# Summing the last four modulation rows on GpSimd: two during the projections, two at half the pace in the attention

## The chip, the cores and the metric

The kernel runs on one core of a Trainium2 chip. The core has TensorE for matmuls (PE in the profile, its weight loads PEld), VectorE (DVE), ScalarE (ACT), GpSimd (POOL) and a queue on SyncE (SP) that here issues all the loads and stores around the change. Each engine works through its own instructions in the order in which the program wrote them. The metric is the device time of one execution in microseconds (us); lower is better.

## The reference

Three layers of a transformer at sequence length 1024 and width 1024. What matters here is the first layer's modulation and what uses it:

```python
mod = jax.nn.silu(c) @ w_ada[l] + b_ada[l]                # c: 1 x 1024, w_ada: 1024 x 6144
shift1, scale1, gate1, shift2, scale2, gate2 = jnp.split(mod, 6, axis=-1)
h = rms_norm(x, norm1_g[l]) * (1.0 + scale1[:, None, :]) + shift1[:, None, :]
z = h @ w_in[l]
c_q, c_kv, k_pe, dq, dk, dv = jnp.split(z, offsets, axis=-1)
...                                                       # MLA attention and differential attention
x = x + gate1[:, None, :] * mix
h2 = rms_norm(x, norm2_g[l]) * (1.0 + scale2[:, None, :]) + shift2[:, None, :]
```

The six rows of `mod` are numbered 0 to 5 in this order. Rows 0 and 1 are needed before the first projection; row 2 (gate1) at the end of the attention, rows 3 and 4 behind it, row 5 (gate2) later still.

## The kernel before

**How a row of the modulation is computed.** A row j needs eight tasks k = 0 to 7. A task loads a 128 x 1024 block of `w_ada` (512 KB, `ada_load`, L588), multiplies it by the column k of silu(c) on GpSimd (one tensor_scalar, L626) and adds it into the accumulator `acc` (`fine`, L335: four adds of 256 columns). Before task 0 the accumulator is zeroed (L582) and its first partition is loaded with the bias (L583). After task 7 TensorE adds up the 128 partitions with a matrix of ones (`ada_sum`, L598, two halves of 512 columns), ScalarE copies the two halves back (L315) and SP stores the row in `d_mod` (L618).

**Double buffers.** The weight blocks have two buffers. The load for task i + 1 is written into the program together with task i, and it overwrites the block of task i - 1. SP therefore waits there until GpSimd has added task i - 1, and everything that stands behind that load in SP's queue waits with it.

**Who sets the order.** `Pipe.feed` is one step of the pipeline: it advances every unit in its list once, in the order of the list, and each unit writes its instructions for that step. A `yield` ends a unit's part of the step. In this text the steps of the q and k projections are numbered: steps 0 to 7 are the calls with `d_unit(0, t)` (L815), steps 8 to 15 those with `d_unit(1, t)` (L828), t = 0 to 7. Ahead of step 0 come the calls with `d_unit(2, t)` (the v projection), behind step 15 those with `latent_unit(t)`.

**The projections** (`phase_z`). In its first step `d_unit(b, t)` writes 24 matmuls of 128 x 512 (L365) into one of four PSUM banks, the copy out of PSUM on ScalarE (L317 or L315) and four VectorE operations of `rope` (L770 to L774). Two steps later come the four transposes (L394) and the split of their result into a high and a low part (L341 on ScalarE, L342 on VectorE) in one of two staging buffers, and one step later the store to `d_dq` or `d_dk` (L795). The weights of the k block are loaded in step 0 by `w_block(1)` (L426, two pieces of 1 MB), ahead of anything that is appended behind `d_unit(0, 0)`. The weights of the latent block are loaded and split in steps 8 to 15. GpSimd has no instruction in the trace between the last row norm of the input and the first norm of the latents.

**The attention** (`phase_attn`). Each pass of the loop (L1163) feeds one `m_unit` and two `d_unit` steps. `ada_rest` is spawned at L1161, waits nine steps (3 * LAG) and then spends two steps on each of its 32 tasks (rows 2 to 5); the row sum is written four steps after the eighth add, by `finish`. Row 2 is read back as `gate` at L1166.

Of the kernel before, what the change touches and what calls it, by code (L numbers as in the profile page):

```python
# [10 lines left out]
F32 = mybir.dt.float32  # L11
# [3 lines left out]
OP = mybir.AluOpType  # L15
# [4 lines left out]
P = 128  # L20
S = 1024
D = 1024
NT = S // P
KD = D // P
# [11 lines left out]
LAG = 3  # L36
# [33 lines left out]
class Pipe:  # L70
# [1 line left out]


    def __init__(self):
        self.active, self.fresh, self.waiting = [], [], []

    def feed(self, *units):
        self.active.extend(self.fresh)
        self.fresh.clear()
        self.active.extend(units)  # L80
        for a in list(self.active):
            if next(a, StopIteration) is StopIteration:
                self.active.remove(a)
        for w in list(self.waiting):
            w[0] = [a for a in w[0] if a in self.active]
            if not w[0]:
                self.waiting.remove(w)
                w[1]()
# [205 lines left out]
def three_layer_kernel(ctx: ExitStack, tc: tile.TileContext, I, out, stop=99, dbg=None):  # L294
    nc = tc.nc
    V, A, G, T, SP = (GUARD(e) for e in (nc.vector, nc.scalar, nc.gpsimd, nc.tensor, nc.sync))
# [9 lines left out]
    go = Pipe()  # L306
# [6 lines left out]
    def acopy(dst, src, scale=None):  # L313
        if scale is None:
            A.activation(out=dst, in_=src, func=AF.Copy)  # L315
        else:
            A.activation(out=dst, in_=src, func=AF.Copy, scale=scale)  # L317
# [14 lines left out]
    def fine(out, a, b, op):  # L332

        for c in range(0, out.shape[-1], 256):
            G.tensor_tensor(out[:, c:c + 256], a[:, c:c + 256], b[:, c:c + 256], op=op)  # L335
# [78 lines left out]
    def weights(raws, parts, per=1):  # L414


        if not raws.rings:
            raws.reserve("raw", 2048)
        nb = len(raws.rings["raw"][0])
        q = []  # L420

        def load(i):
            hi, lo, src = parts[i][:3]
            raw = raws.tile([P, 2048], F32, name="raw")[:, :math.prod(hi.shape[1:])].rearrange(
                "p (k n) -> p k n", k=hi.shape[1])
            SP.dma_start(out=raw, in_=src)  # L426
            q.append(raw)

        for i in range(min(nb, len(parts))):
            load(i)  # L430
        yield
        yield
        for i in range(len(parts)):
            split_k(parts[i][0], parts[i][1], q[i], parts[i][3] if len(parts[i]) > 3 else None)
            if (i + 1) % per == 0 and i + 1 < len(parts):
                yield
            if i + nb < len(parts):
                load(i + nb)
# [4 lines left out]
    def new_weight(name, n):  # L443

        return [new_piece(name, q, n) for q in range(2)]

    def drop_weight(name):
        sb.drop(*[f"{name}{q}{nm}" for q in range(2) for nm in "hl"])

    def halves(pieces, src, c0, n):  # L450
        return [(*pieces[q], wsrc(src, 4 * q, 4, c0, n)) for q in range(2)]
# [42 lines left out]
    d_mod = dp.tile([6, D], F32, name="d_mod")  # L494
# [85 lines left out]
    def ada_acc(j, pl, e):  # L580
        acc = pl.tile([P, D], F32, name="acc", bufs=2)
        e.memset(acc, 0.0)  # L582
        SP.dma_start(out=acc[0:1], in_=I["b_ada"][0:1, j * D:(j + 1) * D])  # L583
        return acc

    def ada_load(pl, j, k):
        w = pl.tile([P, D], F32, name="adaw")
        SP.dma_start(out=w, in_=I["w_ada"][0][k * P:(k + 1) * P, j * D:(j + 1) * D])  # L588
        return w
# [4 lines left out]
    def ada_sum(acc, m=P):  # L594
        res = []
        for c in range(2):
            ps = p_tr.tile([P, 512], name="adaps")[0:m]
            T.matmul(ps, lhsT=ones[:, 0:m], rhs=acc[:, c * 512:(c + 1) * 512], start=True, stop=True)  # L598
            res.append(ps)
        return res  # L600

    def ada_rest():

        ad = Rings(sb, 2)
        todo = [(j, k) for j in range(2, 6) for k in range(KD)]
        w = ada_load(ad, *todo[0])
        accs = {}
        ad.reserve("acc", D, 2)
        for _ in range(3 * LAG):
            yield  # L610

        def finish(j):
            for _ in range(4):
                yield
            for c, ps in enumerate(ada_sum(accs[j], 1)):
                acopy(accs[j][0:1, c * 512:(c + 1) * 512], ps)
            yield
            SP.dma_start(out=d_mod[j:j + 1], in_=accs[j][0:1])  # L618
            if j == 5:
                ad.close()  # L620

        for i, (j, k) in enumerate(todo):
            w2 = ada_load(ad, *todo[i + 1]) if i + 1 < len(todo) else None
            if k == 0:
                accs[j] = ada_acc(j, ad, G)
            G.tensor_scalar(w, w, cc[:, k:k + 1], None, op0=OP.mult)  # L626
            yield
            fine(accs[j], accs[j], w, OP.add)
            w = w2
            yield  # L630
            if k == KD - 1:
                go.spawn(finish(j))

    def phase_z():
        zc = Rings(sb)
# [9 lines left out]
        def w_block(b):  # L645
            W[b] = new_weight(f"w{b}", 512)
            yield from weights(raws, halves(W[b], I["w_in"][0], 576 + 512 * b, 512))
# [14 lines left out]
        acc = [adap.tile([P, D], F32, name="acc", bufs=2) for _ in range(2)]  # L662
# [65 lines left out]
        for q in range(4):  # L728
            w = adap.tile([P, 2, 512], F32, name="adaw")
# [76 lines left out]
            go.feed(*([h_unit(i)] if i < NT else []), *([d_unit(2, i - 4)] if i > 4 else []))  # L806
        hb.close()
        drop_weight("w2")
        go.spawn(w_block(1))
        stg.reserve("qsb", 768)  # L810
        stg.reserve("kn", 512, 1)
# [109 lines left out]
        go.after(done)  # L921

    phase_z()
    if stop <= 1:
        go.drain()
# [51 lines left out]
    def phase_attn(wo, following):  # L977
# [29 lines left out]
        todo = Todo()  # L1007
# [150 lines left out]
        load_v("d", 0)  # L1158
        go.after(start_m)
        go.feed()  # L1160
        go.spawn(ada_rest())  # L1161
        seq = [(h, g, qi) for h in range(4) for g in range(4) for qi in range(2)]
        for i in range(len(seq) + LAG):  # L1163
            if i >= LAG:
# [764 lines left out]

    wo1 = OutWeights(I["w_out"][0], "wo")  # L1930
    w_units = phase_attn(wo1, lambda: open_w(wo1))
    if stop <= 2:
        go.drain()
# [453 lines left out]
```

## Time and profile before

| | us |
|---|---|
| median of 3 runs | 2597.66 |
| lowest and highest run | 2596.23, 2602.85 |
| the profiled execution | 2597.42 |
| span of its trace | 2595.7 |

| engine | busy us | share of the span |
|---|---|---|
| PE | 2461.7 | 95% |
| DVE | 1798.1 | 69% |
| ACT | 1458.0 | 56% |
| POOL | 557.7 | 21% |

The shares are averages over stages with different limits, so the stages are read one by one: the q and k projections, the latents, the attention. The rows below give times in us from the start of the span. In a timeline a row is a run of instructions of one line, with its start, its length, the count behind "x" and, in brackets, the idle time before it and what ended that. An engine's queue is marked with a q (SPq).

### The profile page before, as it was taken

How to read it: one execution, taken by the hardware profiler on the slowest of the kernel's cores; microseconds unless marked ns; L12 is line 12 of the kernel's file. 1: busy time of each engine (PE TensorE's matmuls, PEld its weight loads, DVE VectorE, ACT ScalarE, POOL GpSimd, SP SyncE). 2: the span in 40 equal slices, each digit the busy share in tenths (PEclk: the TensorE clock that was granted, in tenths of full speed). 3: DMA queues.
4: the chain of work that ended last, by engine and by line, in shares of the span. 5: the costliest groups of instructions: out<-in, count | busy, mean ns of one | idle time of the engine just before them, and what ended most of it. 6: DMA issues, size and time to landing. Idle time of an engine off the chain costs nothing. (4 is left out here: it accounts for less than half of the span.)

```text
span 2595.7 us, 37353 instructions
## 1 busy us (share of the span) xinstructions
PE 2461.7 (95%) x13658; PEld 2053.3 (79%) x13658; DVE 1798.1 (69%) x3072; ACT 1458.0 (56%) x2557; POOL 557.7 (21%) x523
## 2 busy tenths in 40 slices
PE   5999899998988999999997999999999899999999
PEld 3789788887876777777765887899999789888977
DVE  7654588887668999999998354536888436735952
ACT  3324577777217878878874343436888224435930
POOL 0000089936002222222211012310002002300400
PEclk8999999999989999999998999999999899999999
DMA  7355765553748999999968524337667324338523
GB/s 267 114 140 164 231 195 162 172 185 110 255 162 307 384 390 386 385 380 382 381 245 315 166 89 147 112 111 198 165 171 204 114 85 147 118 110 190 148 73 106
DMA packets 270416, 530.04 MB, mean 204 GB/s; under 512 B 28027, under 2 KB 180603, under 8 KB 244118
## 3 DMA queue, kind: packets, MB, share of 16 engines
q1 hardware_dynamic: 263062, 510.84, 60.0%
q0 software_dynamic: 7168, 16.79, 1.9%
q8 instruction: 109, 1.79, 0.3%
q14 instruction: 77, 0.63, 0.1%
HBM read 424.19 MB, written 111.76 MB: 206 GB/s over the span
## 5 line engine op out<-in xcount | busy, mean ns | idle before, releaser
L365 PE MATMUL ps<-t,t 128*128 128x512 f32 (+5 forms) x8224 | 1758.3, 370 | 3.8 <-DVE t L342 2.4
L365 PEld LDWEIGHTS ps<-t,t 128*128 128x128 f32 (+1 forms) x8224 | 1377.0, 182 | 313.0 <-DVE t L342 4.4
L342 DVE TENSOR_TENSOR t<-t,t 128x2048 fp32r<-128x2048 f32 (+4 forms) x226 | 472.3, 2115 | 55.3 <-ACT t L341 55.2
L341 ACT ACTIVATE t<-ps 128x512 fp32r<-128x512 f32 (+3 forms) x660 | 334.2, 544 | 313.9 <-PE ps L377 205.1
L342 DVE TENSOR_TENSOR t<-ps,t 128x512 fp32r<-128x512 f32 (+3 forms) x660 | 391.8, 623 | 89.7 <-ACT t L341 83.2
L341 ACT ACTIVATE t<-t 128x2048 fp32r<-128x2048 f32 (+4 forms) x226 | 399.9, 1773 | 31.0 <-DVE t L774 10.9
L322 POOL TENSOR_TENSOR small<-small 128x8 f32<-128x8 f32 (+3 forms) x120 | 137.3, 1145 | 944.8 <-DVE small L321 912.2
L317 ACT ACTIVATE t<-ps,small 96x512 f32<-96x512 f32 (+5 forms) x208 | 128.6, 618 | 322.8 <-PE ps L365 278.0
L335 POOL TENSOR_TENSOR t<-t,t 128x256 f32<-128x256 f32 (+1 forms) x224 | 166.3, 774 | 27.1 <-DMA t<-in_b_ada_dram 23.3
L315 ACT ACTIVATE t<-ps 128x256 f32<-128x256 f32 (+4 forms) x196 | 88.4, 453 | 125.0 <-PE ps L365 69.9
L377 PE MATMUL ps<-small,t 96*128 96x96 f32 (+1 forms) x736 | 94.3, 267 | 47.4 <-DMA t<-d_ye 18.0
L1512 POOL DMA_INDIRECT d_ye<-t,small x32 | 45.2, 1413 | 435.7 <-ACT t L317 429.1
L377 PEld LDWEIGHTS ps<-small,t 96*128 96x128 f32 (+1 forms) x736 | 82.4, 145 | 68.1 <-DVE t L1880 18.5
L2129 DVE TENSOR_TENSOR t<-t,ps 128x512 f32<-128x512 f32 x32 | 22.0, 688 | 125.8 <-PE ps L365 125.8
L2047 DVE CUSTOM_DVE_ANT_0 t<-ps,t 128x1024 f32<-128x1024 f32 (+7 forms) x128 | 95.5, 747 | 19.5 <-PE ps L2042 17.6
L349 DVE SCALAR_TENSOR_TENSOR t<-t,small,t 128x512 fp32r<-128x512 f32 (+5 forms) x124 | 80.2, 692 | 35.7 <-ACT t L348 35.7
L2051 ACT ACTIVATE t<-t,small 128x1024 f32<-128x1024 f32 (+7 forms) x128 | 99.3, 776 | 7.7 <-DVE small L2047 5.4
L626 POOL TENSOR_SCALAR t<-t,small 128x1024 f32<-128x1024 f32 x32 | 92.6, 2894 | 31.9 <-DMA t<-in_w_ada_dram 31.9
L1508 POOL DMA_INDIRECT t<-d_h,small x32 | 89.0, 2781 | 37.5 <-DVE small L1216 28.0
L1090 PE MATMUL ps<-t,t 128*128 128x512 f32 x320 | 83.6, 408 | 8.1 <-ACT t L1136 7.6
L1709 DVE TENSOR_REDUCE small<-t 128x8 f32<-128x512 f32 (+1 forms) x56 | 36.2, 647 | 79.0 <-ACT t L1708 79.0
L2066 PE MATMUL ps<-small,t 128*128 128x128 f32 x576 | 86.2, 277 | 0.4 <-ACT t L2051 0.3
(296 smaller groups left out, 2966.9 us busy)
## 6 DMA issues: line engine op xcount, KB each, us to landing
t<-in_w_expert_gate_dram SPq DMA_DIRECT2D x64, 1024.0 KB, 11.6
t<-in_w_expert_up_dram SPq DMA_DIRECT2D x64, 1024.0 KB, 11.1
t<-in_w_expert_down_dram SPq DMA_DIRECT2D x64, 1024.0 KB, 10.5
t<-in_w_ada_dram SPq DMA_DIRECT2D x48, 512.0 KB, 5.2
t<-d_ak SPq DMA_DIRECT2D x64, 256.0 KB, 4.7
t<-in_w_in_a_dram SPq DMA_DIRECT2D x12, 1024.0 KB, 9.1
t<-in_x_dram SPq DMA_DIRECT2D x16, 512.0 KB, 5.4
t<-d_dk SPq DMA_DIRECT2D x16, 512.0 KB, 8.7
```

The source lines that it names most:

```text
L315: A.activation(out=dst, in_=src, func=AF.Copy)
L317: A.activation(out=dst, in_=src, func=AF.Copy, scale=scale)
L322: G.tensor_tensor(dst, dst, mhalf[:, :dst.shape[-1]], op=OP.pow)
L335: G.tensor_tensor(out[:, c:c + 256], a[:, c:c + 256], b[:, c:c + 256], op=op)
L341: A.activation(out=hi, in_=src, func=AF.Copy)
L342: e.tensor_tensor(lo, src, f(hi), op=OP.subtract)
L365: T.matmul(ps, lhsT=a(k), rhs=b(k), start=(first and i == 0), stop=(last and i == n - 1))
L377: T.transpose(ps[:, k], src[:, (c + k) * P:(c + k + 1) * P], ident[:m, :m])
L626: G.tensor_scalar(w, w, cc[:, k:k + 1], None, op0=OP.mult)
L1508: G.indirect_dma_start(out=xg[e % 3], out_offset=None, in_=d_h2, in_offset=rows(idx_in[:CAP, e:e + 1]), bounds_check=S - 1, oob_is_err=False)
L2047: V.tensor_tensor_reduce(sbt[:, :n], ps[:, :n], c[:, :n], -1.0, 3e38, OP.add, OP.min, nm)
L2051: A.activation(out=pt[:, :n], in_=sbt[:, :n], func=AF.Exp, scale=-1.0, bias=nm, accum_out=RS[h][:, qt:qt + 1])
```

## The change

`Pipe` gets a second list, `side`. `feed` advances its units after all the active ones, so what they write stands behind the step's other instructions on each engine. `ada_rest` now takes the rows that it computes, a number of steps to wait at the start, and the number of steps that each task takes. It is called twice. For rows 2 and 3 it is appended just before step 0 of the projections, with no wait and one step for each task; `more=1` puts tasks 0 and 1 of row 2 into the same step, so that 16 tasks lie in steps 0 to 14. For rows 4 and 5 it is appended where `ada_rest` was before, with the same nine steps of waiting and four steps for each task. A task's product and its add are written into one step. There is one accumulator for both rows of a call. The row sum, its copies and the store of the row are written in the next step after the task with k = 7 (in the projections: steps 7 and 15), in front of the zeroing for the second row. The arithmetic of each task is as before.

```diff
@@ class Pipe
     def __init__(self):
-        self.active, self.fresh, self.waiting = [], [], []
+        self.active, self.fresh, self.waiting, self.side = [], [], [], []
@@ Pipe.feed
         for a in list(self.active):
             if next(a, StopIteration) is StopIteration:
                 self.active.remove(a)
+        for a in list(self.side):
+            if next(a, StopIteration) is StopIteration:
+                self.side.remove(a)
@@ three_layer_kernel
-    def ada_rest():
+    def ada_rest(js, start, pause, more=0):
 
         ad = Rings(sb, 2)
-        todo = [(j, k) for j in range(2, 6) for k in range(KD)]
+        todo = [(j, k) for j in js for k in range(KD)]
         w = ada_load(ad, *todo[0])
-        accs = {}
-        ad.reserve("acc", D, 2)
-        for _ in range(3 * LAG):
-            yield
-
-        def finish(j):
-            for _ in range(4):
-                yield
-            for c, ps in enumerate(ada_sum(accs[j], 1)):
-                acopy(accs[j][0:1, c * 512:(c + 1) * 512], ps)
-            yield
-            SP.dma_start(out=d_mod[j:j + 1], in_=accs[j][0:1])
-            if j == 5:
-                ad.close()
-
+        ad.reserve("acc", D, len(js) - more)
+        acc = ad.tile([P, D], F32, name="acc")
+        for _ in range(start):
+            yield
         for i, (j, k) in enumerate(todo):
             w2 = ada_load(ad, *todo[i + 1]) if i + 1 < len(todo) else None
             if k == 0:
-                accs[j] = ada_acc(j, ad, G)
+                G.memset(acc, 0.0)
+                SP.dma_start(out=acc[0:1], in_=I["b_ada"][0:1, j * D:(j + 1) * D])
             G.tensor_scalar(w, w, cc[:, k:k + 1], None, op0=OP.mult)
-            yield
-            fine(accs[j], accs[j], w, OP.add)
+            fine(acc, acc, w, OP.add)
             w = w2
-            yield
+            if i or not more:
+                for _ in range(pause):
+                    yield
             if k == KD - 1:
-                go.spawn(finish(j))
+                for c, ps in enumerate(ada_sum(acc, 1)):
+                    acopy(acc[0:1, c * 512:(c + 1) * 512], ps)
+                SP.dma_start(out=d_mod[j:j + 1], in_=acc[0:1])
+        ad.close()
@@ phase_z, ahead of go.spawn(w_block(1))
         drop_weight("w2")
+        go.side.append(ada_rest((2, 3), 0, 1, 1))
@@ phase_attn
-        go.spawn(ada_rest())
+        go.side.append(ada_rest((4, 5), 3 * LAG, 4))
```

## Rows read from the trace of the kernel before

**Rows 1.** Windows: projections, attention under ada_rest (length; busy PE, PEld, DVE, ACT, POOL; clock; DMA; GB/s)
```profile
84.00:190.00 106.00, 106.00 (x500) 87.77 (x499) 56.05 (x100) 27.08 (x44) 0.00 (x0) 1.00 0.43 123
330.00:546.00 216.00, 204.60 (x1257) 174.04 (x1258) 188.68 (x297) 167.88 (x325) 191.53 (x168) 0.99 0.64 188
```
**Rows 2.** Timeline of PE in the projections: steps 7 and 15 end, latents begin
```profile
137.24 5.74 PE L365 MATMUL ps<-t,t 128*128 128x512 f32 x24
142.82 0.60 PE L394 MATMUL ps<-small,t 128*128 128x128 f32 x4
...
190.15 0.60 PE L394 MATMUL ps<-small,t 128*128 128x128 f32 x4
190.51 6.63 PE L365 MATMUL ps<-t,t 128*128 128x288 f32 x48
```
**Rows 3.** POOL's groups by line from 320 to 560 us (busy us, mean ns | idle before)
```profile
L335 POOL TENSOR_TENSOR t<-t,t 128x256 f32<-128x256 f32 x128 | 96.0, 780 | 25.1 <-DMA t<-in_b_ada_dram 23.3
L626 POOL TENSOR_SCALAR t<-t,small 128x1024 f32<-128x1024 f32 x31 | 89.7, 2895 | 21.3 <-DMA t<-in_w_ada_dram 21.3
```
**Rows 4.** Timelines of POOL and SP where one modulation row ends, the next begins
```profile
375.50 2.81 POOL L335 TENSOR_TENSOR t<-t,t 128x256 f32<-128x256 f32 x4
378.25 0.96 POOL L582 MEMSET t<- 128x1024 f32 x1
379.18 2.86 POOL L626 TENSOR_SCALAR t<-t,small 128x1024 f32<-128x1024 f32 x1
...
382.70 2.82 POOL L335 TENSOR_TENSOR t<-t,t 128x256 f32<-128x256 f32 x4
...
379.23 0.25 SPq L583 DMA_DIRECT2D t<-in_b_ada_dram  x1
```
**Rows 5.** SP: timeline of the k weights' loads; summary of the q and k stores
```profile
98.53 1.71 SPq L426 DMA_DIRECT2D t<-in_w_in_dram  x2
...
L795 SPq EVENT_SEMAPHORE  x13: 17/17/17, 100.3 to 194.4; - x13
...
DMA to landing us min/median/max: 3.5/4.7/5.8
```
**Rows 6.** Windows, columns as in rows 1: the DMA while the k weights load
```profile
104.00:108.00 4.00, 4.00 (x22) 3.31 (x21) 0.87 (x2) 0.49 (x2) 0.00 (x0) 1.00 0.89 344
108.00:112.00 4.00, 4.00 (x19) 3.31 (x18) 3.80 (x5) 2.39 (x3) 0.00 (x0) 1.00 0.05 16
```
**Rows 7.** Timelines of PE and ACT: one row sum and its second copy
```profile
389.20 1.88 PE L598 MATMUL ps<-t,small 128*1 128x512 f32 x4
...
391.11 0.59 ACT L315 ACTIVATE t<-ps 1x512 f32<-1x512 f32 x1 [0.27 <-PE ps L598]
```
**Rows 8.** Windows, columns as in rows 1: the clock after PE had stood idle
```profile
309.00:319.00 10.00, 4.88 (x15) 3.78 (x16) 4.12 (x8) 4.70 (x8) 0.00 (x0) 0.52 0.96 292
```
**Rows 9.** Timeline of DVE in one step of the projections
```profile
108.13 0.76 DVE L770 TENSOR_TENSOR t<-t,t 128x256 f32<-128x256 f32 x2 [3.23 <-ACT t L317]
109.66 0.69 DVE L774 TENSOR_TENSOR t<-t 128x512 f32<-128x512 f32 x1
```
**Rows 10.** Timelines of DVE and POOL: one meeting, and the same DVE form alone
```profile
341.20 2.12 DVE L1150 SCALAR_TENSOR_TENSOR t<-t,small,t 128x1024 f32<-128x1024 f32 x1
566.05 1.28 DVE L1150 SCALAR_TENSOR_TENSOR t<-t,small,t 128x1024 f32<-128x1024 f32 x1
...
341.12 2.86 POOL L626 TENSOR_SCALAR t<-t,small 128x1024 f32<-128x1024 f32 x1
```
**Rows 11.** Timeline of DVE: row maximum of m_unit in passes 2, 22 and 28
```profile
343.33 1.23 DVE L1098 TENSOR_REDUCE small<-ps 128x1 f32<-128x1024 f32 x1
...
547.16 1.20 DVE L1098 TENSOR_REDUCE small<-ps 128x1 f32<-128x1024 f32 x1
...
606.25 1.20 DVE L1098 TENSOR_REDUCE small<-ps 128x1 f32<-128x1024 f32 x1
```
**Rows 12.** Waits of the SP queue from 288 to 560 us (total, times, longest)
```profile
SPq L588 <- POOL t L335: 140.6, 30, 8.0
```

## The prediction

> **What bounds the kernel now.** I read the windows by stage first. In the projections TensorE is busy without a gap, 106.00 of 106.00 us, VectorE half the time and GpSimd not at all; in the attention under ada_rest TensorE has 204.60 of 216.00, VectorE 188.68, and GpSimd 191.53 [rows 1]. So the projections are set by TensorE alone, and whatever makes it wait there comes out at the end in full; no later stage starts from anything else. The attention is close to TensorE's bound, with VectorE and GpSimd both near 90%. The timeline of PE gives the pace of the projections: a unit of 24 matmuls and 4 transposes starts every (190.15 - 142.82) / 8 = 5.92 us [rows 2]. The timeline of POOL gives the price of a modulation task, the SP rows when its first data can come, and the row maxima of m_unit the pace of the attention.
>
> **The price of a task, and the pace it is given.** 128 adds kept GpSimd busy 96.0 us, so 3.00 us for the four of one task; 31 products took 89.7 us, 2.89 each [rows 3]. A task is 5.89 us; undisturbed it is 2.81 + 2.86 = 5.7 [rows 4]. The change gives it 5.92 us (one step). That looks like a fit, but the first step holds two tasks, and the row sum stands only one step behind the eighth add: eight tasks must end within what TensorE needs for steps 0 to 7, counted from when the first data is there.
>
> **When GpSimd can start.** Step 0 is TensorE's work before step 1; the transposes at 142.82 follow step 7's matmuls, so step 7 is 137.24 to 142.82 [rows 2], and counting back it is 96 to 102 for step 0. Its SP instructions stand in this order: the last v store, the two 1 MB loads of the k weights, then the new loads. SP issues the k weights at 98.53 and is through at 100.3, where its next wait begins [rows 5]. Only then can it issue the first `w_ada` block. The DMA is moving the k weights at 344 GB/s until 108 and is empty behind it (16 GB/s) [rows 6]. The block queues behind them: 0.5 MB at 344 GB/s is 1.5 us more, so it is there at about 110. Bounds: 105 if it is served in between, 112 if bias and second block delay it. I take 110.
>
> **The new wait at step 7.** Eight tasks from 110: 110 + 8 x 5.89 = 157.1. In TensorE's queue the sum of row 2 stands behind step 7's matmuls, which end at 142.8. TensorE waits there 14.3 us, and every later matmul of the kernel is queued behind it. Part of it may show earlier: SP's load for task i + 1 waits for task i - 1, and the q store behind it waits too. The store of unit 0 would go out after the add of task 2 (110 + 3 x 5.89 = 127.7), land 4.7 us later [rows 5] at 132.4, and free the staging buffer that the split of step 4 (119.5) needs. ScalarE, held there, copies out the next banks late, and TensorE may wait some 5 us at the transposes of step 6. That wait lies inside the 14.3 us, since GpSimd does not depend on it.
>
> **The second row.** With one accumulator, GpSimd's zeroing for row 3 waits for the store of row 2, and all the later tasks stand behind it in its queue. After the eighth add: sum and two copies 391.11 + 0.59 - 389.20 = 2.5 us [rows 7]; the 4 KB store 0.25 us to issue and a landing that the trace doesn't show; zeroing 0.96 [rows 4]; product 2.89 and add 3.00. For the landing, the bias load of 4 KB issued at 379.23 was there by 382.70 [rows 4], so at most 3.5 us, and above 0; I take 2.5, nearer to the upper end, since the 512 KB stores took 3.5 to 5.8 [rows 5]. Together 12.1 us until row 3's first add is done, while the bias load hides behind the product. Seven more tasks: 41.2. So the eighth add of row 3 is done at 157.1 + 12.1 + 41.2 = 210.4. TensorE by itself is there at 157.1 + 1.9 [rows 7] + 8 x 5.92 = 206.4, and later by what the clock costs: in ten microseconds of which TensorE was busy for 4.88 the granted clock was 0.52, near the 1.2 GHz level [rows 8], and such a stretch loses 4.8 us; with a third of that it is 208, with all of it 211. Either way the sum of row 3 starts at about 210.5 and the latents at 212.4 instead of 190.5 [rows 2]. **The projections lose 21.9 us**, 3.8 of it the work of the two sums.
>
> What else moves here: 16 loads of 512 KB, two bias loads and two stores join SP's queue, all in front of the k stores and the latent weights' loads of the next step. The latent weights are needed only after step 15 and have some 3 us to spare by the same reckoning. VectorE's rope operations take 0.76 + 0.69 + 0.69 us a step, the third as the second [rows 9]; they will be lengthened by GpSimd as L1150 is, from 1.28 to 2.12 [rows 10]. Four such are at most 3.4 us, and rope ends at 109.66 + 0.69 = 110.35 where the transposes that need it come at 142.82 - 5 x 5.92 = 113.2: 2.9 us of cover. Costed at nothing; without cover, 0.5 us a step, and GpSimd is the later one anyway.
>
> **The attention.** Two of four sums leave it: -3.8 us [rows 7]. At half the density VectorE meets GpSimd half as often. Passes 2 to 22 lie under ada_rest and hold three sums: (547.16 - 343.33 - 3 x 1.88) / 20 = 9.91 us a pass; passes 22 to 28 hold one sum and none of the tasks: (606.25 - 547.16 - 1.88) / 6 = 9.54 [rows 7, 11]. All of the tasks cost 0.37 x 20 = 7.5 us; half of them gives back 3.7. Bounds: 0 and 7.5, with another 1 to 2 us since SP no longer stands 140.6 us waiting for adds [rows 12]: with four steps to a task the add that a load waits for is long done. The new sum stands four steps behind its add, and TensorE doesn't wait there.
>
> **The sum**, against the profiled execution (2597.4, 0.2 below the median, span 2595.7): 2597.4 + 21.9 - 3.8 - 3.7 = 2611.8, say **2612**.
>
> **A rule of the skill.** At 341.20 VectorE's L1150, with two inputs in SBUF, ran into a GpSimd product that began at 341.12 and ran 2.86 us; it took 2.12 us instead of 1.28 [rows 10] and ended at 343.32, before the product did. The Trainium skill, SBUF — State Buffer, "Who interferes with whom", says that the port shared by the two engines is an exclusive lock: the one that comes second is blocked until the first is through. This trace disagrees: the wait was 0.84 us, not 2.8.
>
> **Rivals.** (1) *VectorE's operations hold GpSimd back in full.* Each step has 0.76 + 0.69 + 0.69 = 2.14 us of rope [rows 9]; a task becomes 5.7 + 2.14 = 7.8 us, the sums come at 110 + 63 = 173 and 173 + 14 + 55 = 242, the latents at 244: +53.5 - 7.5, **2643**. Against it: in the attention, where VectorE was 87% busy, the task rose only from 5.7 to 5.89 [rows 3]. Chance 0.04. This is what the lock of the Trainium skill's page, SBUF — State Buffer, would do if VectorE always came first.
> (2) *The blocks come late.* SP's waits and the latents' loads stretch the task to 6.6 us, as the 21.3 us that 31 products waited for data in the attention would (0.7 each) [rows 3]: 110 + 53 = 163, + 12.8 + 46.2 = 222, latents at 224: +33.5 - 7.5, **2623**; at 7.0 us a task it is 2630. Chance 0.14.
> (3) *GpSimd keeps up, and the attention pays back: faster.* It decides at one point: if the eighth add is done by 142.8, TensorE doesn't wait. Then the sums only change places and the attention gains 3.7 to 9 us: **2589 to 2594**. That needs a start at 142.8 - 8 x 5.7 = 97 or before, and SP is through with the k weights only at 100.3 [rows 5]. Chance 0.05.
> (4) *A short wait and a large gain.* Start at 105, tasks of 5.7, store in 0.5 us: eighth adds at 151 and 201, TensorE itself at 202 with a little lost to the clock, latents at 204; +13.5 - 3.8 - 9 = **2598**; in between, no measurable difference. For it: the undisturbed pace does occur [rows 4]. Chance 0.11.
>
> **How the numbers follow.** The forecast has 0.66 and spans 2603 to 2619 by start (105 to 112), store and attention gain. What a measurement of this kernel can tell from no change is about 0.3%, 7.8 us, so faster is below 2589.9 and slower above 2605.5. Slower takes rivals 1 and 2 and nearly all of the forecast: 0.83; same takes rival 4, the lowest part of the forecast and part of rival 3: 0.13; faster, 0.04. The range runs from half of rival 4 to most of rival 2: 2600 to 2627.
>
> **What the profile would show.** PE with a wait at L598 for POOL's L335 near 143 and a second, shorter one near 205; the sum of the PE gaps up to the latents some 18 us; the latents beginning near 212; POOL back to back from about 110 with one hole of about 6 us between the rows; a lower granted clock behind the first wait; the passes of the attention at about 9.7 us. Wrong if L598 shows no wait, if POOL starts before 100, or if passes fall to 9.3.

## The result, and the profile after

The changed kernel took 2617.99 us (median of 4 runs, 2615.82 to 2618.84) against 2600.10 us for the kernel before on the same chip (4 runs, 2596.23 to 2602.85): ratio 1.0067, 95% interval 1.0053 to 1.0082. It is slower by 18 us; the forecast's sum has 14.4. The profiled execution took 2615.82 us, its span is 2614.1, which is 18.4 more than the span of before.

Line numbers moved by a few: the add is now L338 (L335 before), the product L619, the zeroing L617, the load L591, the row sum L601, the matmuls L368, the transposes L397, the q and k stores L792, rope's last operation L771, ScalarE's split L344, the row maximum L1096.

The timeline of PE through the projections, with the idle time and its releaser in brackets:

```profile
140.98 1.09 PE L397 MATMUL ps<-small,t 128*128 128x128 f32 x4 [9.38 <-DVE t L771]
141.72 7.50 PE L368 MATMUL ps<-t,t 128*128 128x512 f32 x24
...
149.41 5.70 PE L368 MATMUL ps<-t,t 128*128 128x512 f32 x24
159.36 3.45 PE L601 MATMUL ps<-t,small 128*1 128x512 f32 x4 [4.24 <-POOL t L338]
...
206.37 0.63 PE L397 MATMUL ps<-small,t 128*128 128x128 f32 x4 [1.99 <-DVE t L771]
206.75 7.33 PE L368 MATMUL ps<-t,t 128*128 128x512 f32 x24
...
218.33 3.57 PE L601 MATMUL ps<-t,small 128*1 128x512 f32 x4 [4.24 <-POOL t L338]
...
222.59 2.61 PE L368 MATMUL ps<-t,t 128*128 128x288 f32 x13
```

Each row sum is met by a wait in two pieces, one at the transposes of an earlier step (9.38, 1.99) and one at the sum itself (4.24 twice), 19.85 us together. The latents begin at 222.59, where it was 190.51 before [rows 2]: 32.1 us later.

The timeline of POOL shows why the sum comes so late:

```profile
109.98 2.86 POOL L619 TENSOR_SCALAR t<-t,small 128x1024 f32<-128x1024 f32 x1 [12.08 <-DMA t<-in_w_ada_dram]
112.92 3.98 POOL L338 TENSOR_TENSOR t<-t,t 128x256 f32<-128x256 f32 x4
116.89 3.29 POOL L619 TENSOR_SCALAR t<-t,small 128x1024 f32<-128x1024 f32 x1
120.26 4.49 POOL L338 TENSOR_TENSOR t<-t,t 128x256 f32<-128x256 f32 x4
...
157.70 2.97 POOL L338 TENSOR_TENSOR t<-t,t 128x256 f32<-128x256 f32 x4
164.79 0.95 POOL L617 MEMSET t<- 128x1024 f32 x1 [4.12 <-DMA d_mod<-t]
...
168.66 3.17 POOL L338 TENSOR_TENSOR t<-t,t 128x256 f32<-128x256 f32 x4
...
178.81 4.46 POOL L619 TENSOR_SCALAR t<-t,small 128x1024 f32<-128x1024 f32 x1
...
216.59 3.04 POOL L338 TENSOR_TENSOR t<-t,t 128x256 f32<-128x256 f32 x4
```

GpSimd starts at 109.98 (forecast 110) and then never waits for a block. Eight tasks end at 157.70 + 2.97 = 160.67, 6.34 us each; the zeroing waits 4.12 us for the store of row 2; the first add of row 3 is done at 171.83, the eighth at 219.63, so 47.8 / 7 = 6.83 us a task.

The timelines of SP and ACT show how the first wait came to stand at the transposes:

```profile
116.94 14.33 SPq L591 DMA_DIRECT2D t<-in_w_ada_dram  x3
131.37 0.53 SPq L792 DMA_DIRECT2D d_dq<-t  x1
...
136.99 0.60 ACT L344 ACTIVATE t<-ps 128x512 fp32r<-128x512 f32 x1 [16.54 <-DMA d_dq<-t]
```

SP sat at a `w_ada` load that needs an add done; the q store behind it left only at 131.37; ScalarE's split waited for the staging buffer, and VectorE's rope and TensorE's transposes waited for ScalarE.

In the attention, the windows from the row maximum of pass 2 to that of pass 22 and on to pass 28, for the kernel before and then for the changed one (the columns as in [rows 1]):

```profile
343.34:547.16 203.82, 194.62 (x1212) 166.60 (x1212) 178.89 (x282) 157.84 (x305) 179.54 (x158) 1.00 0.66 194
547.16:606.25 59.09, 58.09 (x365) 50.03 (x364) 50.26 (x87) 47.61 (x93) 19.68 (x26) 1.00 0.27 93
```

```profile
377.87:569.09 191.22, 189.47 (x1205) 165.90 (x1203) 165.21 (x281) 155.66 (x303) 96.10 (x83) 1.00 0.55 160
569.09:626.53 57.44, 56.71 (x366) 50.18 (x364) 50.08 (x84) 46.41 (x91) 19.11 (x25) 1.00 0.33 111
```

Pass 2 comes 34.5 us later than before, pass 28 only 626.53 - 606.25 = 20.3 later: the attention gives back 14.2 us, where 7.5 was forecast. Another 1.9 us went between there and the end of the span (20.3 to 18.4).

### The profile page after: what moved, and what is told of

Its sections match the earlier page's. It is cut to its first block, busy times and chain, and to the rows that moved or that the text cites. A ratio compares the mean times of both kernels' runs of the same rounds, so it can differ in the third digit from the quotient of the medians.

```text
span 2614.1 us, 37344 instructions
## 1 busy us (share of the span) xinstructions
PE 2468.4 (94%) x13658; PEld 2056.8 (79%) x13658; DVE 1798.1 (69%) x3072; ACT 1458.9 (56%) x2557; POOL 571.2 (22%) x523
## 5 line engine op out<-in xcount | busy, mean ns | idle before, releaser
L368 PE MATMUL ps<-t,t 128*128 128x512 f32 (+5 forms) x8224 | 1760.7, 371 | 4.5 <-DVE t L345 2.9
L368 PEld LDWEIGHTS ps<-t,t 128*128 128x128 f32 (+1 forms) x8224 | 1379.8, 183 | 313.5 <-DVE t L345 5.3
L344 ACT ACTIVATE t<-ps 128x512 fp32r<-128x512 f32 (+3 forms) x660 | 334.6, 544 | 352.4 <-PE ps L380 205.2
L344 ACT ACTIVATE t<-t 128x2048 fp32r<-128x2048 f32 (+4 forms) x226 | 400.0, 1774 | 47.3 <-DMA t<-in_w_in_dram 15.7
L338 POOL TENSOR_TENSOR t<-t,t 128x256 f32<-128x256 f32 (+1 forms) x224 | 178.2, 827 | 31.4 <-DMA t<-in_b_ada_dram 26.3
L380 PEld LDWEIGHTS ps<-small,t 96*128 96x128 f32 (+1 forms) x736 | 83.7, 147 | 67.3 <-DVE t L1878 18.6
L619 POOL TENSOR_SCALAR t<-t,small 128x1024 f32<-128x1024 f32 x32 | 95.2, 2975 | 22.7 <-DMA t<-in_w_ada_dram 22.7
## 6 DMA issues: line engine op xcount, KB each, us to landing
t<-in_w_expert_up_dram SPq DMA_DIRECT2D x64, 1024.0 KB, 10.2
```

The source lines that it names most:

```text
L344: A.activation(out=hi, in_=src, func=AF.Copy)
L368: T.matmul(ps, lhsT=a(k), rhs=b(k), start=(first and i == 0), stop=(last and i == n - 1))
L380: T.transpose(ps[:, k], src[:, (c + k) * P:(c + k + 1) * P], ident[:m, :m])
```

## The experiments

Ratios are to the kernel before, timed on the same chip, with 95% intervals. "Passes 2 to 28" is the time between those two row maxima. Each row sum in it costs 1.88 us [rows 7]; what is left above the kernel without any tasks (e5) is called the cost of the tasks. The changed kernel, e3, e4 and e10 have the same attention, and their passes 2 to 28 take 248.7, 249.2, 248.9 and 249.2 us, so a difference of one microsecond can be read there. Start times are less sure: ahead of the first edited instruction the traces already lie up to 2 us apart. The same eight transposes, in the kernel before and then in e9:

```profile
84.62 1.04 PE L377 MATMUL ps<-small,t 128*128 128x128 f32 x8
...
86.32 1.04 PE L380 MATMUL ps<-small,t 128*128 128x128 f32 x8
```

In most of these kernels the lines have moved once more: the product is L626, rope's last operation L783.

**e3_gq: the loads of rows 2 and 3 on GpSimd's queue.** No q or k store can then stand behind a waiting load.

```diff
-    def ada_load(pl, j, k):
+    def ada_load(pl, j, k, e=SP):
...
-        SP.dma_start(out=w, in_=I["w_ada"][0][k * P:(k + 1) * P, j * D:(j + 1) * D])
+        e.dma_start(out=w, in_=I["w_ada"][0][k * P:(k + 1) * P, j * D:(j + 1) * D])
...
-        go.side.append(ada_rest((2, 3), 0, 1, 1))
+        go.side.append(ada_rest((2, 3), 0, 1, 1, e=G))
```

> The changed kernel, but the w_ada blocks of rows 2 and 3 are loaded from GpSimd's own queue, so SP never stands waiting for an add. Theory A (GpSimd's chain sets the end: first data at 110, tasks of 6.3 to 6.8 us, the row sum right behind the eighth add): the 9.4 us wait of the transposes (L397 there) goes, but the wait at the row sum grows from 4.2 to some 14 us; the latents begin at 222 within 4 us as before, total 2614 to 2622. Rival B (SP standing in front of the q stores is the loss; GpSimd would be nearly in time): both waits shrink, latents near 207, total near 2603.

Measured 2621.47 us, ratio 1.0076 (1.0055 to 1.0097). All of PE's waits before the latents:

```profile
164.49 3.57 PE L601 MATMUL ps<-t,small 128*1 128x512 f32 x4 [19.14 <-POOL t L338]
225.80 3.58 PE L601 MATMUL ps<-t,small 128*1 128x512 f32 x4 [9.91 <-POOL t L338]
```

The waits at the transposes are gone, and all of the wait stands at the sums. It is longer than the 14 us that I expected, and the latents begin at 230.07, not near 222. With GpSimd issuing the loads itself (0.6 us each, and 0.3 of waiting before it), tasks 1 to 7 take 7.36 us each, where it is 6.25 in the changed kernel, and the kernel takes longer too. The first block is there at 100.70, ahead of the k weights, but the first add still comes at 110, as it waits for the bias, which SP loads behind them:

```profile
110.17 4.12 POOL L338 TENSOR_TENSOR t<-t,t 128x256 f32<-128x256 f32 x4 [6.61 <-DMA t<-in_b_ada_dram]
```

So the stores held behind SP's loads only chose the place of the wait; its length is GpSimd's chain.

**e1_row2_late: only row 2 in the projections, its sum five steps later.** Rows 3 to 5 run in the attention at three steps for a task.

```diff
-        go.side.append(ada_rest((2, 3), 0, 1, 1))
+        go.side.append(ada_rest((2,), 0, 1, 1, late=5))
...
-        go.side.append(ada_rest((4, 5), 3 * LAG, 4))
+        go.side.append(ada_rest((3, 4, 5), 3 * LAG, 3))
```

> Only row 2 in the projections, with the same pace and buffers, its sum written five steps later (step 12); rows 3 to 5 in the attention at three steps a task. Theory A: no wait at the row sum, GpSimd is done near 161 and TensorE comes at 172 or later; what SP holds back stays, a wait of up to 9 us at the transposes of step 6 plus 2 to 4 us of lower clock; latents at 190.5 + 1.9 + 9 + 3 = 204, attention gains 1.9 and some 5 of the 10 us that half density gave; total 2600 + 14 - 7 = 2607. Rival B': the wait at the transposes was only the sum's wait in another place and goes with it: latents near 194, total near 2597.

**e2_row2_late_gq: the same, with row 2's loads on GpSimd's queue** (the edits of e1 and e3 together, `e=G` for row 2 alone).

> As e1_row2_late, with the blocks of row 2 loaded from GpSimd's queue. Theory A: neither wait is left; latents at 190.5 + 1.9 + at most 1 = 193; total 2600 + 3 - 7 = 2596, so 8 to 12 us below e1. If TensorE still waits at the transposes, VectorE's lengthened rope is the cause and not the stores: then e2 equals e1.

e1 took 2605.49 us, ratio 1.0019 (1.0008 to 1.0030); e2 took 2595.62 us, ratio 0.9984 (0.9972 to 0.9997). PE's waits from 90 to 235 us (total, times, longest), e1 and then e2:

```profile
PE ps L397 <- DVE t L783: 9.5, 1, 9.5
PE ps L368 <- ACT t L351: 2.3, 1, 2.3
```

```profile
PE ps L368 <- ACT t L351: 2.3, 1, 2.3
PE ps L397 <- ACT t L318: 0.7, 1, 0.7
```

The 2.3 us stand in the latents of the kernel before as well. Five steps of patience remove the wait at the sum; but in e1 the held q store now costs 9.5 us by itself, since nothing later covers it. With the loads off SP that goes too, and the two kernels lie 9.9 us apart. So there are two waits that overlap in the changed kernel, and each must be removed by its own means. With row 2 alone the latents begin at 195.1 in e2, 4.6 us later than before; 1.4 of it are there at the eight transposes already, so the row costs some 3 us, 1.9 of it the sum.

**e7_no_rope: the q and k units without `rope`.** Of the VectorE operations with which a task can meet, rope goes and the splits of the weights stay. With other q and k the data of the later stages changes, so the total is not comparable.

```diff
-            rope(z, z, t, 8, tmp)
```

> The changed kernel with the rope of the differential q and k left out (four VectorE operations a step with both inputs in SBUF; the output is another). Theory C (these operations lengthen GpSimd's tasks from 5.7 to 6.3 and 6.8): tasks near 5.75, eighth add near 156 instead of 160.7, the second row's near 208 instead of 219.6, latents near 210 instead of 222, total 2605 to 2609. Rival D (the lengthening has another cause, as DMA or ScalarE traffic): tasks stay at 6.3 and above, latents at 220 or later, total 2615 to 2619.

The total came to 2695.78 us, and what I expected of it was wrong for that reason: this trace has one expert block more than that of the changed kernel (33 for 32). Rows of POOL's timeline, from row 2's task 0 to the end of its task 7, and one of VectorE's splits of the k weights:

```profile
112.20 4.84 POOL L626 TENSOR_SCALAR t<-t,small 128x1024 f32<-128x1024 f32 x1 [12.68 <-DMA t<-in_w_ada_dram]
117.12 4.88 POOL L338 TENSOR_TENSOR t<-t,t 128x256 f32<-128x256 f32 x4
121.98 2.85 POOL L626 TENSOR_SCALAR t<-t,small 128x1024 f32<-128x1024 f32 x1
...
159.16 2.77 POOL L338 TENSOR_TENSOR t<-t,t 128x256 f32<-128x256 f32 x4
...
112.02 2.29 DVE L345 TENSOR_TENSOR t<-t,t 128x2048 fp32r<-128x2048 f32 x1 [12.00 <-ACT t L344]
```

Tasks 1 to 7 take 159.16 + 2.77 - 121.98 = 39.95 us, 5.71 each, the undisturbed price; in the changed kernel the same seven take 160.67 - 116.89 = 43.78, 6.25 each. Row 3's seven take 6.08 on the mean instead of 6.83, with products of 3.95 and 3.12 where the latents' weights are split. But task 0 takes 9.78 us here and 6.91 in the changed kernel: its product and its adds meet the two splits of the k weights. So row 2 as a whole is hardly shorter (49.7 us, 50.7 in the changed kernel), and the times that I expected were missed: its eighth add comes at 161.93 (156 expected), row 3's at 215.38 (208), the latents at 217.74 (210). VectorE's rope operations and its splits of weights together are what stretched the tasks to 6.34 and 6.83 us; in row 3 rope has 0.75 us of the 1.12 a task, in row 2 the two shares are not separated.

**e4_attn_rows45 and e5_attn_none: the attention alone.** e4 leaves rows 2 and 3 out (their bias is stored in `d_mod`) and keeps rows 4 and 5 at half the density; e5 leaves out all four. The edit of e4 (e5 has `bias_only(2, 3, 4, 5)` and no `ada_rest` there):

```diff
-        go.side.append(ada_rest((2, 3), 0, 1, 1))
...
+        bias_only(2, 3)
         go.side.append(ada_rest((4, 5), 3 * LAG, 4))
```

> The attention's half of the change alone: rows 4 and 5 at four steps a task; rows 2 and 3 are left out (only their bias is stored). If the two halves add up, the projections are as before (latents at 190.5) and passes 2 to 28 of the attention are 14 us shorter than before, 3.8 of it the two sums that are left out: total 2601 - 14 = 2587, with up to 4 us either way from the clock in the router. If the attention's gain came from its later start, it is less than 8.

> Rows 2 to 5 all left out (only their bias is stored). Theory T (what the tasks cost in the attention appears only when GpSimd has no idle time left, as in the kernel before; at half density they cost nothing): passes 2 to 28 are shorter than in e4_attn_rows45 by the two sums only, 3.8 us: total 2583. Rival P (each task costs the same wherever it stands: 10.2 us for the 16 that were taken out, so as much for the 16 left): another 10 us, total 2573.

e4: 2582.67 us, ratio 0.9936 (0.9917 to 0.9954); e5: 2577.59 us, ratio 0.9911 (0.9893 to 0.9930). In e4 the latents begin 0.8 us later than before, which is there ahead of the projections already, and passes 2 to 28 take 248.9 us where it was 262.9: the second half of the change alone is worth 14.0 us. That is the 14.2 of the changed kernel, so its two halves add up. The total of e5 lies between the two theories (2583 and 2573); its passes 2 to 28 decide, 4.2 us shorter than e4's, where theory T has 3.8. The windows of e5, as above:

```profile
342.31:529.41 187.10, 185.57 (x1197) 165.87 (x1196) 160.20 (x281) 153.56 (x299) 6.96 (x10) 1.00 0.46 134
529.41:587.02 57.61, 56.66 (x365) 50.10 (x363) 50.27 (x86) 46.40 (x91) 19.08 (x25) 1.00 0.28 90
```

Without tasks and sums passes 2 to 22 take 187.10 / 20 = 9.36 us each, and passes 22 to 28 take 9.60: TensorE itself is busy longer there (56.66 / 6 = 9.44 us a pass against 9.28), and GpSimd has 19 us of other work. The tasks of before cost 262.91 - 4 x 1.88 - 244.71 = 10.7 us; those at four steps cost 248.66 - 2 x 1.88 - 244.71 = 0.2.

**e6_attn_dense and e11_dense_late: is it the pace or the number?** Both take the changed kernel and give rows 4 and 5 two steps for a task again; e11 also writes both sums four steps behind the last add.

```diff
-        go.side.append(ada_rest((4, 5), 3 * LAG, 4))
+        go.side.append(ada_rest((4, 5), 3 * LAG, 2))
```

> The changed kernel with rows 4 and 5 at two steps a task, so the same 16 tasks at full density in the first half of their time. If the pace is what costs (theory T, 10.6 us for 32 tasks at this pace and 0.4 us for 16 at half of it), passes 2 to 28 are some 5 us longer than in the changed kernel, total near 2623. If the number of tasks is what costs, they are the same, total 2618.

e6 took 2629.36 us, ratio 1.0118 (1.0096 to 1.0140), more than either theory said. Its passes 2 to 28 are 8.1 us longer than in the changed kernel, but one row of PE's timeline holds over half of that:

```profile
415.06 2.72 PE L601 MATMUL ps<-t,small 128*1 128x512 f32 x3 [4.56 <-POOL t L338]
```

At two steps for a task GpSimd is behind when the sum is written, and TensorE waits. So e6 alone does not tell the two apart; it shows that at four steps, with the sum four steps behind its add, this wait stays out of the attention. e11 removes it:

> The changed kernel, with rows 4 and 5 in the attention at two steps a task again, but both row sums written four steps behind the last add, out of two accumulators; so TensorE has no sum to wait for, as it had in the run with the dense halves before this. Theory T (the pace costs: VectorE and GpSimd meet more often in each pass): passes 2 to 28 take some 5 us more than in the changed kernel, 2623 in total. Theory N (only the number of tasks counts, each pays the same at any pace): passes 2 to 28 as in the changed kernel, to 1 us, 2618. No wait of TensorE for POOL at the row sum in either.

2621.40 us, ratio 1.0087 (1.0067 to 1.0108), with no wait at a sum (`ada_rest((4, 5), 3 * LAG, 2, late=4)`, one accumulator for each row); its passes 2 to 28 take 251.9 us against 248.7. The denser pace costs 3.2 us for 16 tasks. That is nearer to theory T than to N, and less than T's 5. Of the 10.5 us that the tasks gave back, 10.7 - 3.4 = 7.3 come with half the number at the old pace, and 3.2 with the slower pace; the first part also holds what it is worth to write product and add into one step, which no run separates.

**e8_before_gq: the kernel before, with its loads on GpSimd's queue.** SP's 140.6 us of waiting for adds [rows 12] are meant to go.

```diff
-        w = ada_load(ad, *todo[0])
+        w = ada_load(ad, *todo[0], G)
...
-            w2 = ada_load(ad, *todo[i + 1]) if i + 1 < len(todo) else None
+            w2 = ada_load(ad, *todo[i + 1], G) if i + 1 < len(todo) else None
```

> The kernel before with the w_ada blocks of rows 2 to 5 loaded from GpSimd's own queue, so SP no longer stands 140 us behind adds. Theory SP (the attention's cost at full density is SP standing in front of its q, k and v loads and stores): most of the 10 us comes back, total 2591 to 2594. Rival V (it is GpSimd's work itself, its full queue and VectorE's lengthened operations): nothing comes back, and 0.6 us of issue in each task costs GpSimd more: total 2600 to 2606.

2619.35 us, ratio 1.0078 (1.0055 to 1.0102), far above what I expected from any theory. Waits of PE and of DVE from 300 to 640 us (total, times, longest):

```profile
PE ps L1071 <- DVE t L1067: 17.6, 10, 6.0
...
DVE small L1065 <- POOL small L322: 13.2, 5, 6.0
```

In the kernel before, the first of them was 2.6 us in all. GpSimd also computes a small norm (L322) on which the attention's output waits; with 0.6 us more for each of 32 tasks the norm stands behind a full queue. And SP's waits did not go: it now waits 60.9 us at the bias loads for GpSimd's zeroing, which was 1.4 before. So e8 does not settle what SP's waits cost; it shows what an over-full queue of GpSimd does. The 10.7 us of the kernel before are no single wait. PE's longest waits in its passes 2 to 28:

```profile
PE ps L1090 <- ACT t L1136: 3.9, 9, 0.9
PE ps L1017 <- DVE t L1150: 1.8, 5, 0.4
PE ps L1071 <- DVE t L1067: 1.6, 3, 0.8
```

In e5 the first is 2.0 us, the second 0.4 and the third not there. All of TensorE's idle time is 10.2 us here and 2.5 in e5, and VectorE is busy 229.2 us for what takes it 210.5 in e5.

**e9_attn4_25 and e12_attn4_25_s9: all four rows in the attention at 2.5 steps a task.** If a pace of four steps makes tasks nearly free, a somewhat slower pace without the projections should gain. e9 starts at once (0 in place of the 9 in the last line), e12 after the nine steps of before.

```diff
-        go.side.append(ada_rest((2, 3), 0, 1, 1))
...
-                for _ in range(pause):
+                for _ in range(pause + i % 2):
...
-        go.side.append(ada_rest((4, 5), 3 * LAG, 4))
+        go.side.append(ada_rest((2, 3, 4, 5), 9, 2))
```

> All four rows in the attention, none in the projections, from its first step on and two and three steps a task in turn (2.5 instead of 2), with the sum right behind the last add. Theory T: GpSimd gets idle time, most of the 10 us comes back without any loss in the projections: total 2592 to 2595. Rival P (the number of tasks counts, not their density): total 2600 to 2602. If the sum waits for the eighth add, that shows at the sum's line, some 1 to 4 us each.

> All four rows in the attention, none in the projections, at two steps for a product and three for the next by turns (2.5 on the mean), as in an earlier run that measured 2596, but with the start after nine steps as in the kernel before instead of at once. There TensorE lost some 4 us ahead of the attention's first passes. If the early start, with its loads and products beside the latents' tail, was the cause, that loss goes: 2592 to 2594, some 7 us under the kernel before. If the loss has another cause, 2596 as in that run. The attention's passes 2 to 28 some 5 us shorter than in the kernel before in either case.

e9 took 2596.02 us, ratio 0.9983 (0.9973 to 0.9992); e12 took 2593.75 us, ratio **0.9965 (0.9951 to 0.9979)**, 7.7 us under the kernel before. The row of PE's timeline where the attention's first scores begin, e9 and then e12:

```profile
311.20 0.79 PE L1136 MATMUL ps<-t,t 128*128 128x512 f32 x1 [4.91 <-ACT t L1145]
```

```profile
306.86 0.50 PE L1136 MATMUL ps<-t,t 128*128 128x512 f32 x1 [2.76 <-ACT t L1145]
```

In e9 pass 2 comes 4.0 us later than before, in e12 0.1. Of the 4.0, 1.7 are there at the eight transposes (84.62 and 86.32), ahead of any edit; the early start cost the other 2.3. Passes 2 to 28 take 257.6 and 256.9 us, 5.3 and 6.1 less than before. e12 has the lowest ratio of the kernels that compute all four rows, though its interval overlaps those of e9 and e2.

**e10_three_stages: row 2 in the projections, row 3 in the latents at two tasks a step, rows 4 and 5 as in the change**, the loads of rows 2 and 3 on GpSimd's queue.

```diff
-        go.side.append(ada_rest((2, 3), 0, 1, 1))
+        go.side.append(ada_rest((2,), 0, 1, 1, late=5, e=G))
...
+            if t == 2:
+                go.side.append(ada_rest((3,), 0, 1, late=1, pair=1, e=G))
```

> Row 2 in the projections as in e2_row2_late_gq, row 3 during the latents (from their third unit on, two tasks a step of 13 us, loads on GpSimd's queue, the sum two steps behind the last add), rows 4 and 5 in the attention as in the change. From the runs so far: projections +4.6 as in e2, latents +1.9 for the sum and up to 2 for norms of the latents that stand behind tasks on GpSimd, attention -14: total 2600 - 6 = 2594, bounds 2590 and 2599. If the norms wait for more than a step, the latents' gaps show it and it is slower than e2.

2610.35 us, ratio 1.0042 (1.0026 to 1.0059); I had expected a gain. The attention gave back its 14 us, but it began 25.6 us late. One row each of the SP waits, of ACT and of PE in the latents:

```profile
SPq L616 <- ACT t L318: 18.6, 1, 18.6
...
311.09 1.09 ACT L344 ACTIVATE t<-ps 128x512 fp32r<-128x512 f32 x2 [13.12 <-DMA d_mq<-t]
...
312.46 1.11 PE L380 MATMUL ps<-small,t 128*128 128x128 f32 x4 [8.68 <-DVE t L345]
```

The store of row 3's sum waited 18.6 us in SP's queue for ScalarE's copies, and the latents' q store stood behind it: the mechanism of 131.37 again, with another instruction at its head. These 8.68 us are TensorE's longest wait there; the rest of the 25.6 is not taken apart.

The cost of the tasks over passes 2 to 28, from these runs; the first two to six tasks of each begin ahead of pass 2 and are not counted:

| steps for a task | run | tasks counted | cost us | per task |
|---|---|---|---|---|
| 2 (product and add a step apart) | before | 28 | 10.7 | 0.38 |
| 2 | e11 | 13 | 3.4 | 0.26 |
| 2.5 | e9, e12 | 26, 29 | 5.4, 4.6 | 0.21, 0.16 |
| 3 | e1, e2 | 21 | 3.3, 3.1 | 0.16, 0.15 |
| 4 | after, e4 | 14 | 0.2, 0.4 | 0.01, 0.03 |

The windows of e11 and e12 for it (the columns as in [rows 1]):

```profile
376.34:628.20 251.86, 246.93 (x1568) 216.12 (x1566) 217.16 (x365) 202.82 (x394) 107.08 (x103) 1.00 0.48 145
...
343.41:600.27 256.86, 251.28 (x1576) 216.78 (x1576) 225.07 (x367) 204.99 (x398) 203.50 (x186) 1.00 0.59 175
```

So the price of a task falls with the pace. By what path is in part open: SP's waits for adds fall with it too (122.6 us of this stretch in the kernel before, 100.6 in e12, 61.7 in e11, 16.0 in the changed kernel), and no run changes one without the other. But of TensorE's waits in these stretches only 1.3 us, in the kernel before, end with a load; the others end with ScalarE or VectorE.

## Why the prediction was right, point by point

**The start at 110** was right (109.98), and so was the order in SP's queue from which it came: in e3 a block that is issued ahead of the k weights is there at 100.70.

**The new wait at step 7** was right in kind, place and releaser: at L601 for POOL's L338, partly moved ahead to the transposes of step 6 through the held q store, which left at 131.37 (127.7 forecast) and set ScalarE free at 136.99 (132.4 forecast). The part at the transposes was 9.38 us, not some 5; e3 shows that this part is inside the whole, as I argued.

**The length of a task was mis-sized.** I took 5.89 us from the attention [rows 3] and costed VectorE's rope at nothing because TensorE did not need it; its splits of weights are in no term of the price. But the meetings lengthen GpSimd's side too: 6.34 us in row 2 and 6.83 in row 3, so 3.6 us to the first sum and 6.6 more to the second; e7 shows the cause, both together. I should have taken the price from a stage with this VectorE work, or put its operations into the task's price, a quarter to a half of the way from 5.89 to rival 1's 7.8. Rival 2's 6.6 us a task was the right size, but its cause was not: no product after the first waits for its block.

**The gap between the rows** was 171.83 - 160.67 = 11.2 us, 12.1 forecast; the store of row 2, issued at 163.46, let the zeroing start 1.3 us later, where I took 2.75. **The clock**: at the second sum it was low, so that the sum took 3.57 us instead of 1.88; because GpSimd set the pace, the lower clock behind the first wait cost nothing that can be seen at the second. The latents began at 222.6 instead of 212.4: 9.2 us by the tasks and the gap, 1.0 behind the eighth add, where the clock was low. Up to pass 2 another 2.4 us were lost, which I had not counted.

**The attention's gain was mis-sized the other way**, 14.2 us for 7.5. The sums' 3.8 stand. For the tasks I measured passes 2 to 22 against passes 22 to 28 and took the second as the pace without them. It is not: with all tasks left out, they take 9.60 us and passes 2 to 22 take 9.36. Against a run without tasks those of before cost 10.7 us, not 7.5; and half of them at four steps cost 0.2, not half. So 10.5 us came back in place of 3.7. Passes 2 to 22 took (191.22 - 2 x 1.88) / 20 = 9.37 us, not some 9.7, and so nearly the 9.3 that I had named as a sign of being wrong.

**The sum.** Forecast: +21.9 - 7.5 = 14.4 on the span. Measured: 34.5 at pass 2, - 14.2 in the attention, - 1.9 behind it = 18.4. The two errors, 12.6 us too little and 6.7 too much, partly cancel. The path and both signs were as forecast; that the total came out within 4 us is partly luck. That 1.9 us and the 2.4 of the latents have no experiment of their own. Of the rivals, rival 4's large gain in the attention came, but not its short wait; rival 3 needed the eighth add by 142.8, and it came at 160.7.

## What to carry to other kernels

Idle time of an engine is a place for work only if the work's first data can be there in time and its last result isn't asked for at once: here GpSimd was free for the whole stage, and still one sum written too early, or one load at the head of a shared queue, put its lateness on TensorE. Price moved work in the company that it will have, in both directions: list the other engine's operations in that stage and ask which of the two will come first. Take a baseline for "without it" from a run without it, not from other passes of the loop. Spacing the same work out in the stage where it already hides (2.5 steps for 2) gained 0.35%, while moving half of it into the stage where TensorE has no slack lost 0.7%, though the attention gave back 14 us.

## What the runs showed of the hardware

When operations of VectorE and GpSimd with their inputs in SBUF meet, the one that comes second waits, and the two do not wait alike. GpSimd waits nearly to the end: in e7 a product that began 0.18 us after VectorE's split of 128 x 2048 took 4.84 us instead of 2.85, so it lost 2.0 of the 2.1 us that the split still had to run. In all the kept traces 41 of 400 products took 3.05 us or more; 40 of them began while a VectorE operation with both inputs in SBUF was running, the other in the same moment as one. VectorE waits less: its L1150 took 2.12 us instead of 1.28 when it began 0.08 us into a product [rows 10], and only its 1.28 us when it began 1.16 us into one of 2.86, in the kernel before:

```profile
361.25 2.86 POOL L626 TENSOR_SCALAR t<-t,small 128x1024 f32<-128x1024 f32 x1
...
362.41 1.28 DVE L1150 SCALAR_TENSOR_TENSOR t<-t,small,t 128x1024 f32<-128x1024 f32 x1
```

The Trainium skill, SBUF — State Buffer, "Who interferes with whom", has the second engine blocked until the first is through. These traces agree where VectorE comes first and disagree where GpSimd does. Had VectorE always come first, a 2.14 us rope in each step would have made tasks of 5.7 + 2.14 = 7.8 us by rival 1's reckoning, and the runs show 6.34 and 6.83. VectorE's split of the transposes, with one input in PSUM, ran in four of e7's tasks of 5.7 us and lengthened none.

TensorE's clock fell behind each wait. In the windows around the first two waits, the mean granted clock was 0.53 and 0.58, near 1.2 GHz:

```profile
134.50:145.50 11.00, 4.52 (x13) 3.79 (x14) 5.72 (x10) 2.17 (x4) 10.92 (x10) 0.53 0.60 165
158.50:162.50 4.00, 3.14 (x4) 0.29 (x4) 0.00 (x0) 0.59 (x1) 2.17 (x4) 0.58 0.34 103
```

A load issued from GpSimd's own queue cost it 0.6 us of its time in e3, so moving a load off SP is not free when GpSimd is the late one; in e2, with five steps of patience, it was worth 9.9 us.
